# A down GEMM with tokens on the partitions of its result: final norm per partition, residual brought into token order by transfers and VectorE transposes

## The chip, the cores and the metric

The kernel runs on one core of one Trainium2 chip. The metric is the device time of one execution in microseconds (us); lower is better. A core has TensorE (PE; its weight loads are listed as PEld), VectorE (DVE), ScalarE (ACT), GpSimd (POOL), and SyncE (SP), which here only issues transfers. SBUF and PSUM have 128 partitions; a PSUM bank holds 512 float32 values in each partition.

## The reference

The reference computes one step of a one-layer encoder for 1024 prompt tokens and 8 x 16 sample tokens, 1152 in all, with a model width of 1024. The first half of the layer mixes three branches and adds the normed result to the input, which gives `x`. What matters here is the second half:

```python
def rmsnorm(x, g):
    xf = x.astype(F32)
    y = xf * lax.rsqrt(jnp.mean(xf * xf, axis=-1, keepdims=True) + EPS)
    return (y * g.astype(F32)).astype(x.dtype)
...
    h2 = rmsnorm(x, p['g_pre2'])
    f, conv_new = conv_ffn(h2, conv_buf, p['w_ffn_up'], p['w_dw'], p['b_dw'], p['w_ffn_down'])
    x = x + rmsnorm(f, p['g_post2'])
```

`conv_ffn` projects up to 2 x 2816 columns, applies a causal convolution of width 3, GELU and a gate, and projects down again: `act @ w_ffn_down`, a product of 1152 x 2816 by 2816 x 1024. All is float32, and the norm's mean is taken over the 1024 model columns of one token.

## The kernel before

**Layout.** Nearly everything is kept with features on the partitions and tokens along the free axis. The 1152 tokens are three chunks of 384 (`ch(c)`, line 191); the 1024 model columns are eight feature blocks `f` of 128; the 2816 inner columns are 22 blocks `ff`.

**Float32 out of pieces.** A float32 operand is split into a high part, rounded to the format float32r that TensorE multiplies in one pass, and a low part (`split`, line 60: one ScalarE copy and one subtraction on VectorE or GpSimd). `mm3` (line 100) then issues three matmuls: high x high, high x low, low x high. In it, the first operand is the stationary one (128 x 128 weights loaded into TensorE) and the second the moving one, whose columns stream through.

**The up GEMM** (`phase_u`, line 1471). For each `ff` it makes the activation `t` of 128 inner features x 1152 tokens and stores it to the DRAM tile `Dact[ff]` (`up_out`, line 1467). The residual x after the first half, called x2, was stored earlier to the DRAM tile `Dx2[c]`, feature-major (line 1249).

**The down GEMM** (`phase_d`, line 1501). The inner blocks are taken as 2 + 4 x 4 + 4:

- `first()` (line 1649): blocks 0 and 1 for all chunks, with `whole_mm`; the results start the accumulators `M` (seven products) and `y2`.
- four groups of four blocks (`group`, line 1551). For chunks 0 and 1 a group is a 2 x 2 x 2 block product done with seven multiplications (`prod`, line 1615; sums and differences of weight blocks "A" and of activation blocks "B"), and chunk 2 is done plainly (`plain`, line 1632). Each result in PSUM is added into an accumulator in SBUF by `evac` (line 1626), on VectorE. The next group is loaded and split beside it (a Python generator, advanced by `next(nx)`).
- `rest()` (line 1657): the last four blocks, once more with `whole_mm`, in the order chunk 2, 0, 1 and within it over the eight feature blocks (`last_down`, line 1698). Between them the products in `M` are summed into the chunks' results (`sums`, line 1788).

Here the weight slices are stationary (128 inner x 128 model columns) and the activations move (384 tokens), so a result has 128 model columns on its partitions and 384 tokens along the free axis.

**The final norm.** As the model columns lie on the partitions, the sum of squares runs across partitions. `last_down` squares each feature block on ScalarE and adds the squares up on GpSimd; `final_rms` (line 1715) sums over partitions with matmuls against a column of ones and takes the power -1/2 on GpSimd (`rsqrt`, line 79); `row_bcast` (line 88) spreads the 384 factors to all partitions by three diagonal matrices and a matmul with ones; `final_rows` (line 1726) loads x2 in four pieces, multiplies by gain (a value per partition, in `vec`) and by the broadcast row in PSUM, adds x2 on VectorE and GpSimd, and stores `y[c, f]`. For chunks 2 and 0 this goes on beside the matmuls of the next chunk; for chunk 1 it comes after the last matmul. Twelve matmuls whose result is not used (line 1812) stand in the wait.

**What sets the order.** A planner orders each engine's instructions by a simulated timeline: of what is ready by its own estimates it takes the most urgent. `tc.keep_in_program_order` pins an instruction, `tc.high_priority` makes it more urgent, `tc.issue_after(i)` keeps instructions behind `i` on its engine. Nearly all transfers are issued by SP, one queue in order. Results go to eight PSUM banks in turn (`bank`, line 1531).

Of the kernel before, what the change touches and what calls it, by code (L numbers as in the profile page):

```python
# [21 lines left out]
V_PSCALE, V_D, V_WDW, V_BDW, V_GPOST1, V_GPOST2, V_N = 52, 54, 58, 124, 146, 154, 162  # L22
# [9 lines left out]
class K:  # L32
# [75 lines left out]
    def consts(self):  # L108
# [9 lines left out]
        nc.gpsimd.memset(self.mhalf, -0.5)  # L118

# [1347 lines left out]
    def up_out(self, s):  # L1467
        self.nc.vector.tensor_mul(s.t, s.t, s.g)
        self.nc.sync.dma_start(self.Dact[s.ff], s.t)

    def phase_u(self):
        for s in self.first:
# [28 lines left out]
    def phase_d(self):  # L1501
# [6 lines left out]
        with ExitStack() as ctx:  # L1508
            def pool(name, bufs):
                return ctx.enter_context(tc.tile_pool(name=name, bufs=bufs, reuse_waits="tile"))  # L1510
            P = _Multi(pool("d", 1), {"sq": pool("dsq", 3), "tmp": pool("dtm", 2), "dB": pool("db", 1)})
# [19 lines left out]
            def bank():  # L1531
                self.nb += 1
                return (self.sm() if self.nb % 2 else self.pc())[:, 0:384]
# [81 lines left out]
            def prod(s, p):  # L1615
# [16 lines left out]
            def plain(s, f):  # L1632
                b = bank()
                fs = slice(f % 4 * 128, f % 4 * 128 + 128)
                for k in range(4):
                    ah, al = s.A[("A11", "A12", "A21", "A22")[f // 4 * 2 + k // 2]]
                    self.mm3(b, ah[:, k % 2, fs], al[:, k % 2, fs], s.c[:, 0, k], s.c[:, 1, k], k == 0, k == 3)
                evac(False, y2[:, f], b)
# [46 lines left out]
            def whole_mm(ss, c, f, pin=False):  # L1685
                b = bank()
                fs = slice(f * 128, f * 128 + 128)
                for i, s in enumerate(ss):
                    self.mm3(b, s.wh[:, fs], s.wl[:, fs], s.hi[:, self.ch(c)], s.lo[:, self.ch(c)],
# [3 lines left out]
            def row(c, f):  # L1693
                if c == 2:
                    return y2[:, f]
                return M[((2, 4), (3, 5))[c][f // 4]][:, f % 4]

            def last_down(last, c, f, acc, end):

                b = whole_mm(last, c, f, True)  # L1700
                y = row(c, f)
                self.evac = V.tensor_add(y, y, b)
                tc.keep_in_program_order(self.evac)
                if f == 0:
                    nc.scalar.activation(acc[0], y, AF.Square)
                    return
                sq = P.tile([128, 384], F32, tag="sq", name="sq")
                nc.scalar.activation(sq, y, AF.Square)
                if end and f > 5:
                    acc.append(sq)  # L1710
                else:
                    with tc.high_priority():
                        G.tensor_add(acc[0], acc[0], sq)

            def final_rms(acc):
                ss = self.sm()[:, 0:3]
                for i, s in enumerate(acc):
                    for t in range(3):
                        m = nc.tensor.matmul(ss[:, t:t + 1], s[:, t * 128:t * 128 + 128], self.ones[:, 0:1],
                                             start=(i, t) == (0, 0), stop=(i, t) == (len(acc) - 1, 2))  # L1720
                        if i + t == 0:
                            tc.keep_in_program_order(m)
                with tc.high_priority():
                    return self.rsqrt(P, ss, 3)

            def final_rows(c, rs, i):

                with tc.high_priority():
                    rb = self.row_bcast(P, rs, 3, self.pc(), pin=True)
                order = tc.keep_in_program_order  # L1730
                yield
                for f in range(0, 8, 2):
                    if i == 2:
                        x2 = self.rawtile([128, 2, 384], "x2r")
                    else:
                        x2 = self.w2.tile([128, 2, 384], F32, tag="w", name="x2r")
                    nc.sync.dma_start(x2, self.Dx2[c, f:f + 2].rearrange("f p n -> p f n"))
                    y = [row(c, f), row(c, f + 1)]
                    for k in range(2):
                        order(V.scalar_tensor_tensor(y[k], y[k], self.vec[:, V_GPOST2 + f + k:V_GPOST2 + f + k + 1],  # L1740
                                                     rb, op0=OP.mult, op1=OP.mult))
                    order(V.tensor_add(y[0], y[0], x2[:, 0, :]))
                    (V if (i, f) == (3, 6) else G).tensor_add(y[1], y[1], x2[:, 1, :])
# [251 lines left out]
```

## Time and profile before

| | |
|---|---|
| median of 3 runs | 1547.19 us (1545.49 to 1548.5) |
| profiled execution, its own time | 1548.72 us |
| its span, first to last instruction | 1546.9 us |
| mean granted TensorE clock | 0.993 |
| transfers | 183.51 MB, 109,263 packets, mean 119 GB/s |
| last stage (`whole_mm` of the last four blocks) | first matmul at 1477.24 us, last at 1530.46 us |

Times within the profile count from the span's start. A busy share is an engine's time with at least one instruction at work, and a matmul's recorded length overlaps the next one's start, so the pace of matmuls is read from their starts. "Chain" on the page is the work that ended last, followed back from the end:

```profile
PE 83%; DVE 7%; DMA 4%; ACT 3%; issue 2%; POOL 0%; DVEq 0%; ACTq 0%; SPq 0%; POOLq 0%
```

### The profile page before, as it was taken

Reading aid. Unit: us, or ns where it says so; the run is one execution under the profiler, and the core shown is the slowest. Engines: PE = TensorE matmul, PEld = TensorE weight load, DVE = VectorE, ACT = ScalarE, POOL = GpSimd, SP = SyncE. Lnnn points to the kernel's source line nnn. Section 1 sums busy time; section 2 is a strip of 40 time slices with the busy share of each in tenths; the row PEclk is TensorE's granted clock in tenths of the full one; section 3 lists DMA queues with packets and bytes.
Section 4 is the critical chain, followed back from the end, with each engine's and each line's share of the span. In section 5 each row is a group of like instructions: output and inputs, shape, how many; then the busy total and the mean of one; then the engine's idle time right before and its main releaser. Section 6 shows DMA issues by size and latency. Waiting matters only on the chain.

```text
span 1546.9 us, 23088 instructions
## 1 busy us (share of the span) xinstructions
PE 1524.9 (99%) x8914; PEld 1489.2 (96%) x8914; DVE 1097.8 (71%) x1714; ACT 627.4 (41%) x960; POOL 451.4 (29%) x429
## 2 busy tenths in 40 slices
PE   9999999999999899999999999999999999999997
PEld 7999998889999899999999999999999999999997
DVE  7956987796788666637587566566566569888876
ACT  8313445373655224435454343333333343333322
POOL 0000010000012343300046344344344301565545
PEclk9999999999999999999999999999999999999998
DMA  7533334554345873513313221221221233222324
GB/s 270 171 103 103 109 117 161 166 217 125 103 155 171 250 218 103 156 36 123 126 50 117 72 93 70 72 85 57 74 84 57 84 109 133 75 102 98 93 73 167
DMA packets 109263, 183.51 MB, mean 119 GB/s; under 512 B 24417, under 2 KB 76769, under 8 KB 109153
## 3 DMA queue, kind: packets, MB, share of 16 engines
q1 hardware_dynamic: 108576, 181.54, 35.4%
q8 instruction: 70, 1.15, 0.3%
q10 hardware_dynamic: 576, 0.49, 0.1%
q14 instruction: 41, 0.33, 0.1%
HBM read 134.27 MB, written 47.73 MB: 118 GB/s over the span
## 4 chain that ended last, share of the span: by engine, by line
PE 83%; DVE 7%; DMA 4%; ACT 3%; issue 2%; POOL 0%; DVEq 0%; ACTq 0%; SPq 0%; POOLq 0%
PE pc L106 14%; PE pc L102 14%; PE pc L105 14%; PE ps L102 11%; PE ps L105 11%; PE ps L106 11%; DMA Ts<-DG 1%; PE ps L854 1%; DMA DG<-gs 1%; ACT hhi L125 1%; DVE dB L63 1%; PE ps L768 1%; DVE mg L1265 1%; PE ps L1212 0%; PE ps L820 0%
## 5 line engine op out<-in xcount | busy, mean ns | idle before, releaser
L105 PE MATMUL pc<-hlo,whi 128*128 128x384 f32 x504 | 171.8, 341 | 0.3 <-DVE hlo L126 0.3
L102 PE MATMUL pc<-hhi,whi 128*128 128x384 f32 x504 | 171.7, 341 | 0.0
L106 PE MATMUL pc<-hhi,wlo 128*128 128x384 f32 x504 | 169.9, 338 | 0.5 <-DVE wlo L63 0.5
L63 DVE TENSOR_TENSOR wlo<-rawt,whi 128x1024 fp32r<-128x1024 f32 (+1 forms) x99 | 123.0, 1243 | 54.1 <-ACT whi L62 53.8
L62 ACT ACTIVATE whi<-rawt 128x1024 fp32r<-128x1024 f32 (+1 forms) x99 | 103.3, 1044 | 124.8 <-PE pc L105 71.5
L62 ACT ACTIVATE S<-S 128x512 fp32r<-128x512 f32 x112 | 69.9, 629 | 163.8 <-PE ps L106 87.0
L63 DVE TENSOR_TENSOR S<-S,S 128x512 fp32r<-128x512 f32 x112 | 88.9, 798 | 54.9 <-ACT S L62 52.8
L106 PE MATMUL pc<-h2hi,wlo 128*128 128x384 f32 x352 | 119.1, 338 | 0.0
L105 PE MATMUL pc<-h2lo,whi 128*128 128x384 f32 x352 | 118.4, 336 | 0.5 <-DVE h2lo L63 0.5
L102 PE MATMUL pc<-h2hi,whi 128*128 128x384 f32 x352 | 118.5, 337 | 0.0
L102 PE MATMUL ps<-bT,S 128*128 128x384 f32 x304 | 101.7, 334 | 0.0
L105 PE MATMUL ps<-bT,S 128*128 128x384 f32 x304 | 101.7, 334 | 0.0
L106 PE MATMUL ps<-bT,S 128*128 128x384 f32 x304 | 101.7, 334 | 0.0
L105 PEld LDWEIGHTS pc<-hlo,whi 128*128 128x128 f32 x504 | 94.7, 188 | 3.7 <-DVE hlo L126 1.0
L106 PEld LDWEIGHTS pc<-hhi,wlo 128*128 128x128 f32 x504 | 94.7, 188 | 2.9 <-DVE wlo L63 1.2
L102 PEld LDWEIGHTS pc<-hhi,whi 128*128 128x128 f32 x504 | 94.8, 188 | 1.9 <-issue 0.6
L62 ACT ACTIVATE dhi<-dwr 128x1024 fp32r<-128x1024 f32 x38 | 39.6, 1057 | 83.9 <-PE pc L105 49.3
L102 PE MATMUL ps<-ohi,whi 128*128 128x384 f32 x192 | 65.6, 342 | 3.7 <-DVE sgl L1158 2.7
L105 PEld LDWEIGHTS pc<-h2lo,whi 128*128 128x128 f32 x352 | 66.0, 188 | 0.8 <-DVE h2lo L63 0.8
L106 PEld LDWEIGHTS pc<-h2hi,wlo 128*128 128x128 f32 x352 | 66.2, 188 | 0.0
L102 PEld LDWEIGHTS pc<-h2hi,whi 128*128 128x128 f32 x352 | 66.1, 188 | 0.0
L85 POOL TENSOR_TENSOR rs_y<-rs_v,mhalf 128x3 f32<-128x3 f32 (+1 forms) x13 | 14.0, 1081 | 177.2 <-ACT rs_v L83 177.2
(494 smaller groups left out, 4610.8 us busy)
## 6 DMA issues: line engine op xcount, KB each, us to landing
rawt<-in_w_up SPq DMA_DIRECT2D x44, 512.0 KB, 3.4
rawt<-in_w_gate SPq DMA_DIRECT2D x40, 512.0 KB, 3.8
Dsg<-sg SPq DMA_DIRECT2D x72, 192.0 KB, 1.9
sgl<-Dsg SPq DMA_DIRECT2D x72, 192.0 KB, 3.2
Dact<-t SPq DMA_DIRECT2D x22, 576.0 KB, 3.7
dwr<-in_w_down SPq DMA_DIRECT2D x22, 512.0 KB, 3.5
xT<-in_xT SPq DMA_DIRECT2D x20, 384.0 KB, 7.7
dBr<-Dact SPq DMA_DIRECT2D x8, 768.0 KB, 5.2
```

Source lines behind the costliest of these rows:

```text
L62: a = nc.scalar.activation(hi, src, AF.Copy)
L63: return a, (eng or nc.vector).tensor_sub(lo, src, hi)
L85: nc.gpsimd.tensor_tensor(y, v, self.mhalf[:, 0:n], op=OP.pow)
L102: i = nc.tensor.matmul(out, whi, xhi, start=start, stop=False)
L105: nc.tensor.matmul(out, whi, xlo, start=False, stop=False)
L106: nc.tensor.matmul(out, wlo, xhi, start=False, stop=stop)
L125: a = nc.scalar.activation(hi[:, k, :], x[:, k, :], AF.Copy, scale=g)
L768: nc.tensor.matmul(od[:, b, hp, :], cv[:, b % 2, m, hp * 128:hp * 128 + 128], PT[:, 2 * (b // 4) + hp, m, 32 * (b % 4):32 * (b % 4) + 32], ...
L854: nc.tensor.matmul(o, va[:, m, 2 * hp + e, :], pT[:, m, :], start=m == 0, stop=m == 1)
L1265: V.scalar_tensor_tensor(oT[:, f, :], oT[:, f, :], self.vec[:, V_GPRE2 + f:V_GPRE2 + f + 1], rb, op0=OP.mult, op1=OP.mult)
```

## The change

The roles in `mm3` are exchanged throughout the down GEMM: slices of the activations (128 inner x 128 tokens) are stationary and the weights (512 model columns) move. A result has 128 tokens on its partitions and 512 model columns along the free axis: half `h` of token tile `t` of chunk `c`. `prod`, `plain`, `evac`, `whole_mm`, the accumulators and the initial loop follow.

The final norm is then per partition. `square` lets ScalarE square a half and sum it along the free axis (`accum_out`), and turns it into mean + EPS with a second small instruction whose bias is the value of the half before. GpSimd takes the power of one value per partition. The gain is now along the free axis: `g2`, loaded once, 128 equal rows, multiplied in on GpSimd (the last half on VectorE). One VectorE instruction per half multiplies by the factor and adds x2. The last half of the last tile is done in two pieces of 256 columns.

x2 must come in token order. During the up GEMM `x2_blocks` copies `Dx2` to a new DRAM tile `Dx2b`, two copies in each of 18 steps, 36 in all, each 128 KB in runs of 32 tokens; `x2_load` loads a token tile of it and transposes it in blocks of 32 x 32 on VectorE. `final_rms`, `final_rows` and the twelve unused matmuls go. The layout of the output `y` and its rearrangement on the host follow.

```diff
+        self.eps = c.tile([128, 1], F32, name="eps")
+        nc.gpsimd.memset(self.eps, EPS)
...
-        self.nc.sync.dma_start(self.Dact[s.ff], s.t)
+        self.act_out = self.nc.sync.dma_start(self.Dact[s.ff], s.t)
+
+    def x2_blocks(self, n):
+
+        c, t, a = n // 12, n // 4 % 3, n % 4
+        D = self.Dx2[c].rearrange("f p n -> (f p) n").rearrange("(b i) n -> i b n", i=32)
+        at = t * 128 + 32 * a
+        self.nc.sync.dma_start(self.Dx2b[c, t, a].rearrange("i (b j) -> i b j", b=32), D[:, :, at:at + 32])
...
                 self.up_last(cur, "a")
+                with self.tc.issue_after(self.act_out.ins):
+                    for n in range(2 * ff - 6, min(2 * ff - 4, 36)):
+                        self.x2_blocks(n)
...
-            P = _Multi(pool("d", 1), {"sq": pool("dsq", 3), "tmp": pool("dtm", 2), "dB": pool("db", 1)})
+            P = _Multi(pool("d", 1), {"sq": pool("dsq", 2), "dB": pool("db", 1)})
+            g2 = P.tile([128, 1024], F32, tag="g2", name="g2")
+            nc.sync.dma_start(g2, self.I["g2"])
...
-                for f in range(4):
-                    fs = slice(f * 128, f * 128 + 128)
+                for t in range(3):
+                    ts = slice(t * 128, t * 128 + 128)
                     b = bank()
                     for k in range(2):
-                        self.mm3(b, ah[:, k, fs], al[:, k, fs], bh[:, k, :], bl[:, k, :], k == 0, k == 1)
-                    evac(s.g == 0 and p in (1, 5, 6), M[p][:, f], b)
+                        self.mm3(b, bh[:, k, ts], bl[:, k, ts], ah[:, k, :], al[:, k, :], k == 0, k == 1)
+                    evac(s.g == 0 and p in (1, 5, 6), M[p][:, t], b)
...
+            def x2_load(c, t):
+
+                r = self.rawtile([128, 1024], "x2b")
+                nc.sync.dma_start(r, self.Dx2b[c, t].rearrange("a i n -> (a i) n"))
+                x2 = self.w2.tile([128, 1024], F32, tag="w", name="x2r")
+                V.transpose(x2, r)
+                return x2
+
+            def square(y, bias):
+
+                sq = P.tile([128, 512], F32, tag="sq", name="sq")
+                n = y.shape[1]
+                a = small("ss")
+                nc.scalar.activation(sq[:, 0:n], y, AF.Square, accum_out=a)
+                v = small("rs_v")
+                nc.scalar.activation(v, a, AF.Identity, scale=1.0 / 1024, bias=bias)
+                return v
+
+            def last_down(c, t, x2, end):
+
+                v = self.eps
+                yg = []
+                for h in range(2):
+                    y = row(c, h)[:, t]
+                    for cols in (slice(0, 256), slice(256, 512)) if end and h else (slice(0, 512),):
+                        b = whole_mm(cur, c, t, h, True, cols)
+                        self.evac = V.tensor_add(y[:, cols], y[:, cols], b)
+                        tc.keep_in_program_order(self.evac)
+                        v = square(y[:, cols], v)
+                    g = g2[:, 512 * h:512 * h + 512]
+                    if end and h:
+                        z = P.tile([128, 512], F32, tag="yg", name="yg")
+                        V.tensor_mul(z, y, g)
+                        y = z
+                    else:
+                        G.tensor_mul(y, y, g)
+                    yg.append(y)
                 with tc.high_priority():
-                    rb = self.row_bcast(P, rs, 3, self.pc(), pin=True)
...
+                    r = small("rs_y")
+                    G.tensor_tensor(r, v, self.mhalf[:, 0:1], op=OP.pow)
+                for h in range(2):
+                    V.scalar_tensor_tensor(yg[h], yg[h], r, x2[:, 512 * h:512 * h + 512], op0=OP.mult, op1=OP.add)
+                    (nc.scalar if end and h else nc.sync).dma_start(self.O["y"][3 * c + t][:, 512 * h:512 * h + 512], yg[h])
...
+            sums = {(2, 0): ((G, 2, 1), (V, 6, 1)), (2, 1): ((V, 4, 6),), (2, 2): ((V, 4, 7),), (0, 0): ((V, 5, 6),),
+                    (0, 1): ((V, 3, 5),), (0, 2): ((G, 5, 7),)}
+            tiles = [(c, t) for c in (2, 0, 1) for t in range(3)]
+            x2 = [x2_load(*tiles[i]) for i in range(2)]
+            for i, (c, t) in enumerate(tiles):
+                if i + 2 < len(tiles):
+                    x2.append(x2_load(*tiles[i + 2]))
+                last_down(c, t, x2[i], i == len(tiles) - 1)
+                for e, p, q in sums.get((c, t), ()):
+                    e.tensor_add(M[p], M[p], M[q])
```

More of the change, by code (lines that the diff above doesn't have):

```diff
@@ L1690, in whole_mm, with row @@
                              i == 0, i == len(ss) - 1, pin and i == 0)
                 return b
-            def row(c, f):
+            def row(c, h):
                 if c == 2:
[L1695 to L1722, printed above, removed]
-                with tc.high_priority():
-                    return self.rsqrt(P, ss, 3)
@@ L1726, in final_rows @@
-            def final_rows(c, rs, i):
-                with tc.high_priority():
-                    rb = self.row_bcast(P, rs, 3, self.pc(), pin=True)
[L1730 to L1743, printed above, removed]
-                    for k in range(2):
-                        nc.sync.dma_start(self.O["y"][c, f + k], y[k])
-                    yield
+                    return y2[:, :, 512 * h:512 * h + 512]
@@ new lines, in row, with small @@
+                return M[((2, 4), (3, 5))[c][h]]
+            def small(name):
+                return P.tile([128, 1], F32, tag=name, name=name, bufs=3)
+            def x2_load(c, t):
[12 more added lines that the diff above has]
+                return v
@@ L1752, in phase_d @@
             Mt = [self.mtile([128, 2, 4, 384], F32, f"M{i}") for i in range(4)]
+            Mt = [t.rearrange("p i f n -> p (i f n)").rearrange("p (i t n) -> p i t n", i=2, t=3) for t in Mt]
             M = {p: Mt[(p - 1) // 2][:, (p - 1) % 2] for p in range(1, 8)}
[L1754 to L1758 removed]
+            y2 = self.mtile([128, 3, 1024], F32, "y2")
+            for c, h, p in ((0, 0, 2), (1, 0, 3), (1, 1, 7), (0, 1, 4), (2, 0, 0), (2, 1, 0)):
+                for t in range(3):
+                    b = whole_mm(cur, c, t, h)
                     if p == 4:
[L1760 removed]
+                        V.tensor_sub(M[4][:, t], b, M[7][:, t])
                     else:
[L1762 removed]
+                        evac(True, M[p][:, t] if p else row(2, h)[:, t], b)
                 next(nx, None)
@@ L1773, in phase_d @@
                 prod(cur, 2)
-                for f in range(8):
-                    plain(cur, f)
-                    if f % 4 == 3:
-                        next(nx, None)
+                for h in range(2):
+                    for t in range(3):
+                        plain(cur, t, h)
+                    next(nx, None)
                 for p in (3, 4, 5, 6, 7):
@@ L1783, in phase_d @@
                 cur = new
-            accs = Mt[3][:, 1].rearrange("p (c k) n -> p c k n", c=2)
-            acc = [[accs[:, i % 2, 0]] for i in range(3)]
-            rows = iter(())
-            sums = {(0, 0): ((G, 2, 1), (V, 6, 1)), (0, 1): ((V, 4, 6),), (0, 3): ((V, 4, 7),), (0, 4): ((V, 5, 6),),
-                    (0, 6): ((V, 3, 5),), (0, 7): ((G, 5, 7),)}
-            order = (2, 0, 1)
-            for i, c in enumerate(order):
-                for f in range(8):
-                    last_down(cur, c, f, acc[i], i == 2)
-                    for e, p, q in sums.get((i, f), ()):
-                        e.tensor_add(M[p], M[p], M[q])
-                    if i:
-                        if f == 1:
-                            rs = final_rms(acc[i - 1])
-                        elif f == 3:
-                            rows = final_rows(order[i - 1], rs, i)
-                            next(rows)
-                        if 2 < f < (7 if i == 1 else 6):
-                            next(rows)
-            with tc.issue_after(self.evac.ins):
-                rs = final_rms(acc[2])
-                for _ in rows:
-                    pass
-            b = bank()
-            s = cur[0]
-            for _ in range(12):
-                tc.keep_in_program_order(nc.tensor.matmul(b, s.wh[:, 0:128], s.hi[:, 0:384], start=True, stop=True))
-            for _ in final_rows(order[2], rs, 3):
-                pass
+            sums = {(2, 0): ((G, 2, 1), (V, 6, 1)), (2, 1): ((V, 4, 6),), (2, 2): ((V, 4, 7),), (0, 0): ((V, 5, 6),),
[8 more added lines that the diff above has]
+                    e.tensor_add(M[p], M[p], M[q])
 class _S:
@@ L1888, in _layout @@
         cols(a["pool_scale"]), cols(a["ssm_d"][0][perm]), cols(a["w_dw"]), cols(a["b_dw"]),
-        cols(a["g_post1"]), cols(a["g_post2"])], axis=1))
+        cols(a["g_post1"])], axis=1))
+    o["g2"] = c(np.tile(a["g_post2"].reshape(1, 1024), (128, 1)))
     cst = np.zeros((128, C_N), f)
@@ L1960, in _unlayout @@
     y = np.empty((NT, 1024), np.float32)
-    y[_rows()] = r["y"].transpose(0, 3, 1, 2).reshape(NT, 1024)
+    y[_rows()] = r["y"].reshape(NT, 1024)
     mk = r["mk"].reshape(2, 64, 2, 256).transpose(3, 2, 0, 1)
```

32 lines of the change are left out of this document (14 added, 18 removed).

## The prediction

> **What bounds the kernel now.** I read the page's busy shares first, then the table of stretches over the down GEMM, then the timeline of the end. Columns of the stretches: start and end, length, then busy us and instruction count of PE, PEld, DVE, ACT and POOL, granted clock, DMA share, GB/s.
>
> ```profile
> PE 1524.9 (99%) x8914; PEld 1489.2 (96%) x8914; DVE 1097.8 (71%) x1714; ACT 627.4 (41%) x960; POOL 451.4 (29%) x429
> ...
> 1290.00:1300.00 10.00, 9.17 (x53) 8.69 (x51) 10.00 (x17) 4.33 (x5) 0.00 (x0) 1.00 0.00 0
> 1300.00:1335.00 35.00, 34.35 (x195) 33.96 (x195) 29.01 (x40) 9.96 (x10) 11.44 (x6) 1.00 0.38 129
> ...
> 1477.20:1530.60 53.40, 53.30 (x306) 52.10 (x305) 36.69 (x51) 14.04 (x31) 35.47 (x29) 1.00 0.30 96
> 1530.60:1546.90 16.30, 6.65 (x34) 5.95 (x32) 8.70 (x17) 2.21 (x6) 6.13 (x6) 0.68 0.39 147
> ```
>
> TensorE never stops before 1530.6 us, but for 0.8 us and 0.65 us in 1290 to 1335, where VectorE was busy without a break (10.00 of 10). So in the down GEMM only TensorE's own time counts, and after 1530.6 a chain of small steps, 16.3 us long. Its main steps, from the timeline (start, length, engine):
>
> ```profile
> 1530.46 0.33 PE L106 MATMUL pc<-act,dlo 128*128 128x384 f32 x1
> ...
> 1530.83 0.55 DVE L1702 TENSOR_TENSOR M<-M,pc 128x384 f32<-128x384 f32 x1 [0.32 <-PE pc L106]
> ...
> 1531.47 0.52 ACT L1708 ACTIVATE sq<-M 128x384 f32<-128x384 f32 x1 [0.35 <-DVE M L1702]
> ...
> 1532.92 0.17 ACT L83 ACTIVATE rs_v<-ps 128x3 f32<-128x3 f32 x1 [0.92 <-PE ps L1719]
> 1533.73 0.85 POOL L85 TENSOR_TENSOR rs_y<-rs_v,mhalf 128x3 f32<-128x3 f32 x1
> 1534.62 0.99 ACT L93 ACTIVATE diag<-ident,rs_y 128x128 f32<-128x128 f32 x3 [1.53 <-POOL rs_y L85]
> 1536.47 0.81 PE L95 MATMUL pc<-diag,ones 128*128 128x384 f32 x2
> 1537.32 1.14 DVE L1740 SCALAR_TENSOR_TENSOR M<-M,vec,pc 128x384 f32<-128x384 f32 x2 [4.42 <-PE pc L95]
> ...
> 1543.40 0.55 DVE L1743 TENSOR_TENSOR M<-M,x2r 128x384 f32<-128x384 f32 x1
> ```
>
> After the last matmul come the square, column sums on TensorE, the power, three diagonals, a broadcast matmul, and 6.6 us of VectorE over a whole chunk of 384 tokens (1537.32 to 1543.95). From there to the end of the span, 1546.9, it is 2.95 us (the last store and the program's close).
>
> **The matmul stream.** The old form has 1488 matmuls with a moving operand of 384 columns (144 in the first two feature blocks, 264 in each of four groups, 288 in the last four blocks). The new one has 1116 of 512: the same 571,392 columns. So all hangs on whether a matmul has a fixed cost. Starts of back-to-back matmuls at three widths:
>
> ```profile
> 75.26 0.28 PE L102 MATMUL ps<-whi,mhi 128*128 128x256 f32 x1
> ...
> 76.70 0.28 PE L102 MATMUL ps<-whi,mhi 128*128 128x256 f32 x1
> ...
> 321.70 0.40 PE L847 MATMUL ps<-at 128*128 128x512 f32 x1
> ...
> 322.64 0.34 PE L105 MATMUL pc<-hlo,whi 128*128 128x384 f32 x1
> ...
> 323.86 0.33 PE L106 MATMUL pc<-hhi,wlo 128*128 128x384 f32 x1
> ...
> 378.32 0.39 PE L848 MATMUL ps<-at,at 128*128 128x512 f32 x1
> ...
> 379.93 0.34 PE L102 MATMUL pc<-hhi,whi 128*128 128x384 f32 x1
> ```
>
> Between the first pair lie 12 steps of 256 columns, 0.120 us each. From 322.64 to 323.86 are 7 steps of 384: 0.174. From 321.70 to 322.64 are 4 steps of 512 (0.235), from 378.32 to 379.93 seven (0.230): 0.232 over the eleven. Per column 0.453 ns at 384 and 0.453 at 512: 1488 x 0.174 = 258.9 us and 1116 x 0.232 = 258.9 us. I take **0**. The bounds: a straight line through 256 and 384 gives 0.228 at 512, 254.4 us, 4.5 saved; at 0.235 it is 262.3, 3.4 lost. The last half tile in two pieces of 256 costs 24 x 0.120 - 12 x 0.232 = 0.1 more.
>
> The Trainium skill, "TensorE: Matmul & The Clock Gate", section "Back-to-back issue gap", gives columns / 2.4 + 2.5 ns: by it (an estimate) 0.1625 and 0.216, and a gain of 1.0 us. The trace's 0.174 and 0.232 do not agree with it.
>
> **Norm work taken out of the stream.** For chunks 2 and 0 the column sums and the broadcast sat between matmuls of the last stage:
>
> ```profile
> 1498.32 0.34 PE L106 MATMUL pc<-act,dlo 128*128 128x384 f32 x1
> ...
> 1499.55 0.34 PE L106 MATMUL ps<-act,dlo 128*128 128x384 f32 x1
> ...
> 1503.20 0.34 PE L106 MATMUL pc<-act,dlo 128*128 128x384 f32 x1
> ...
> 1504.19 0.33 PE L105 MATMUL ps<-act,dhi 128*128 128x384 f32 x1
> ```
>
> Three ordinary steps took 1.23 us in place of 0.52, and two took 0.99 in place of 0.35: 1.35 us for a chunk. Two chunks: **-2.7**. Nothing replaces it on TensorE, as the sum of squares now comes out of ScalarE's accumulator.
>
> **The prices of the new small steps.** Rows by form (busy us, mean ns):
>
> ```profile
> L580 DVE TENSOR_TENSOR V<-ar,ps 128x512 f32<-128x512 f32 x4 | 2.7, 684 | 0.1
> L1628 DVE COPY M<-ps 128x384 f32<-128x384 f32 x12 | 6.6, 550 | 5.3 <-PE pc L106 5.3
> L63 DVE TENSOR_TENSOR wlo<-rawt,whi 128x1024 fp32r<-128x1024 f32 x97 | 121.6, 1254 | 48.9 <-ACT whi L62 48.5
> L855 DVE RECIPROCAL yt<-ps 64x512 f32<-64x512 f32 x8 | 26.8, 3355 | 1.8 <-PE ps L854 1.6
> L62 ACT ACTIVATE S<-S 128x512 fp32r<-128x512 f32 x112 | 69.9, 629 | 163.8 <-PE ps L106 87.0
> L1399 POOL TENSOR_TENSOR S<-rawt 128x512 f32<-128x512 f32 x19 | 25.6, 1348 | 124.3 <-PE ps L106 124.3
> L1795 POOL TENSOR_TENSOR M<-M 128x1536 f32<-128x1536 f32 x1 | 4.2, 4211 | 0.0
> ```
>
> Taking a result out of PSUM costs VectorE 0.684 at 512 (first row) against 0.550 at 384, so 18 where 24 stood save 24 x 0.550 - 18 x 0.684 = 0.9 us of VectorE in the first stage, where it starved TensorE for 1.5. I take half of it: **-0.4**, between -1.5 (stall gone) and +1.5 (the planner's new order stalls as much again).
>
> **The new end.** Stream end to first step: 1530.46 + 0.174 = 1530.63, so 0.20 to 1530.83. Then, for a last piece of 256 columns: add out of PSUM 0.42 (0.684 and 0.550 carried on to 256); hand-over 0.09 and square 0.42 (from 0.629 and 0.52); the mean with bias 0.10 + 0.17; power 0.10 + 0.85; two final multiply-adds of 512 columns 0.05 + 2 x 0.684. That is 3.8, and with the 2.95 after VectorE's last step 6.7 us. The multiplication of the last half by the gain (VectorE) lies beside the square.
>
> What may be late is GpSimd's queue. A tile of 128 tokens lasts 24 x 0.232 = 5.57 us of TensorE. GpSimd does two gain multiplications and a power in it: 2 x 1.348 + 0.85 = 3.55. The final multiply-add now reads two operands from SBUF, where the old one read the broadcast from PSUM, and such a step does not run beside GpSimd:
>
> ```profile
> 1525.95 1.02 POOL L1713 TENSOR_TENSOR M<-M,sq 128x384 f32<-128x384 f32 x1 [0.52 <-ACT sq L1708]
> ...
> 1526.16 1.23 DVE L1742 TENSOR_TENSOR M<-M,x2r 128x384 f32<-128x384 f32 x1
> ...
> 1532.35 0.55 DVE L1742 TENSOR_TENSOR M<-M,x2r 128x384 f32<-128x384 f32 x1
> ```
>
> The same addition took 0.55 alone and 1.23 where GpSimd was already at work. So the two share 3.55 + 2 x 0.684 = 4.92 of the 5.57. The sum of M5 and M7 on GpSimd, 4.2 us, falls after the sixth of nine tiles, and three tiles recover only 3 x 0.65 = 1.95: some 2.5 us are still owed at the last tile. The tail is then 9.2, between 6.7 (nothing owed) and 12. Against 16.3: **-7.1**, between -9.6 and -4.3.
>
> The Trainium skill, "SBUF — State Buffer", section "SBUF: two separate sides", calls this an exclusive lock held for a whole instruction by a VectorE step with two SBUF inputs or by GpSimd; the 1.23 agrees.
>
> **The transposes.** Nine of 128x1024 on VectorE; the trace has none. Between 1.25 us (the 1024-wide subtraction) and 6.7 (twice the 512-wide reciprocal, the dearest form per column). I take 1.25, as the nearest in kind: each element is read and written once. VectorE then has 2 x 0.684 + 1.25 + 2 x 0.684 = 4.0 a tile, within 5.57, and its sums are done ahead as now; eight PSUM banks, 2.8 us of TensorE each, cover a late one. So 0.
>
> The Trainium skill, "Vector Engine (DVE) Microarchitecture Reference", section 3.8, has a transpose at one element per cycle and lane, at 0.96 GHz an estimated 1.07 us; no run here shows it, and by it the sum is the same.
>
> **The transfers.** 36 copies of 128 KB from DRAM to DRAM in pieces of 128 bytes, two in each of 18 steps of the up GEMM; then nine loads of 512 KB in place of twelve of 384, and one of 512 KB for the gain.
>
> ```profile
> DG<-gs SPq DMA_DIRECT2D x4, 64.0 KB, 3.3
> ...
> 1018.32 0.33 SPq L1469 DMA_DIRECT2D Dact<-t  x1
> 1028.25 0.33 SPq L67 DMA_DIRECT2D rawt<-in_w_up  x1
> ```
>
> The nearest, 64 KB in small pieces, lands in 3.3 us, so two copies are done within 3.3 to 13 us. SP's queue is empty for 10 us behind the store of `Dact` where they go, and they wait for a store of x2 hundreds of us old. Only the next weight load could be held, by 3 us at most, while TensorE is at the products of the block before (it shows no idle time in these stretches): 0. Without that cover each of the 18 steps would pay up to 3 us; I leave that out of the range. The gain's load goes where tiles of the up GEMM lay; should it be queued ahead of the loads behind it, it would hold them, which I price in the range alone.
>
> **Sum.** -2.7 - 7.1 - 0.4 + 0.1 = -10.1. The profiled execution took 1548.72 (span 1546.9), so 1538.6; that run lies 1.5 above the median, 1547.19, and from the median it is **1537.1 us**.
>
> **The rivals.**
> 1. *A fixed cost per matmul* (0.228 at 512): 4.5 more is saved, 1532.6. For it: 256 columns cost 0.469 ns each. Against: the eleven steps of 512. Chance 0.15.
> 2. *GpSimd and VectorE take the tail's place*: the lock and the sums leave 6 us or more owed at the last tile, so that the tail stays at 12 to 16 and little but the norm work is won: 1543, between 1540 and 1547. For it: only 0.65 of 5.57 spare. Against: GpSimd kept up with 35.47 of 53.40 before. Chance 0.18, one half within 0.2% of before.
> 3. *VectorE becomes the bound of the last stage*: transposes at 6.7 make 9.4 a tile, 3.9 over, and nine tiles 35 us, all at the end, as the banks only put it off: 1572. All gains are gone at 10.1 / 9 = 1.1 over, which is a transpose of 3.9 us. For it: no row of a transpose, and the reciprocal shows that a VectorE step can cost five times another. Against: it does no arithmetic. Chance 0.12, slower.
> 4. The forecast: 0.55.
>
> A measurement of this kernel tells about 0.2% (3 us) from no change. Faster: 0.55 + 0.15 + half of 0.18 less a little = 0.78; same 0.10; slower 0.12. The range: low end 1537.1 - 4.5 (stream) - 2.5 (nothing owed) - 1.1 (stall gone) = 1529; high end + 3.4 + 2.8 + 1.9 (first stage) = 1545.2, set to 1546 for part of rival 2.
>
> **What would show it.** Steps of 512 columns at 0.232 in the down GEMM; no gap in the last stage's matmuls; under 10 us from the last matmul to the end; transposes near 1.25; unchanged stretches of the up GEMM. I am wrong if TensorE waits in the last stage for PSUM, if the transposes take over 2.8 us (5.57 less the other steps, 4 x 0.684), or if the planner orders the first stage so that weights come late.

## The result and the profile after

The changed kernel takes 1539.22 us (median of 4 runs, 1536.95 to 1539.43), the kernel before 1547.10 in the runs beside it (1545.49 to 1548.5). The ratio is 0.9944, with a 95% interval from 0.9929 to 0.9958: 8 us faster. The forecast was 1537.1. So the total came out close, but not by the parts that were forecast.

The profiled execution of the changed kernel took 1536.95 us, 2 us less than its other three runs. Two executions differ by some microseconds already before the stages that were changed (the twelve traces reach the same matmul between 783.5 and 788.7 us), so all comparisons of traces below count from one matmul, the first of the up GEMM that reads `h2hi`. From the timeline of TensorE of before, then of after (start, length, engine and line):

```profile
788.28 0.34 PE L102 MATMUL pc<-h2hi,whi 128*128 128x384 f32 x1
```

```profile
784.95 0.34 PE L102 MATMUL pc<-h2hi,whi 128*128 128x384 f32 x1
...
1518.35 0.28 PE L106 MATMUL ps<-dhi,act 128*128 128x256 f32 x1
```

From there to the last matmul are 1530.46 - 788.28 = 742.18 us before and 1518.35 - 784.95 = 733.40 after: **the stream of matmuls lost 8.8 us**, where the forecast had 3.0. From the last matmul to the end of the span are 1546.9 - 1530.46 = 16.4 before and 1535.2 - 1518.35 = 16.8 after: **the tail lost nothing**, where the forecast had 7.1. Together they are 8.4 us, close to the 7.9 of the medians.

The stretches of after, with the columns of the stretches of before. The first two held TensorE's gaps before; the third is the turn from the groups to the last stage, which TensorE begins at 1468.57; the fourth is the rest of that stage, the fifth what follows the last matmul:

```profile
1290.00:1300.00 10.00, 10.00 (x46) 8.29 (x45) 10.00 (x14) 0.85 (x1) 0.00 (x0) 1.00 0.40 138
1300.00:1335.00 35.00, 35.00 (x154) 28.53 (x153) 29.97 (x37) 11.65 (x12) 17.95 (x8) 1.00 0.26 89
...
1463.00:1479.00 16.00, 16.00 (x71) 12.97 (x70) 15.73 (x17) 1.17 (x1) 0.00 (x0) 1.00 0.56 193
1479.00:1518.50 39.50, 39.50 (x184) 32.67 (x182) 34.98 (x34) 13.63 (x42) 29.09 (x21) 1.00 0.29 109
1518.50:1535.20 16.70, 0.13 (x2) 0.00 (x0) 7.39 (x12) 4.00 (x15) 6.38 (x7) 0.64 0.25 95
```

TensorE (first pair) has no gap left, neither at 1290 to 1335 nor in the last stage. VectorE (third pair) has none either from 1463 to 1479, 15.73 of 16: it enters the last stage late, and takes the stage's first result out of PSUM 8.1 us behind the last matmul of that result (bare of the norm, 4.1). In the kernel before it was 3.8 us behind there, and had caught up by the sixth feature block (0.4). What it does in the tail is seen in the timeline of the end (in brackets the idle time before an instruction, and who ended it):

```profile
1519.16 0.55 POOL L1757 TENSOR_TENSOR rs_y<-rs_v,mhalf 128x1 f32<-128x1 f32 x1
1519.74 1.41 DVE L1759 SCALAR_TENSOR_TENSOR M<-M,rs_y,x2r 128x512 f32<-128x512 f32 x2 [2.65 <-POOL rs_y L1757]
1521.08 0.68 DVE L1744 TENSOR_TENSOR M<-M,ps 128x512 f32<-128x512 f32 x1
1521.67 0.68 DVE L1744 TENSOR_TENSOR M<-M,pc 128x512 f32<-128x512 f32 x1
1521.79 0.63 ACT L1731 ACTIVATE sq<-M 128x512 f32<-128x512 f32 x1 [3.61 <-DVE M L1744]
...
1522.59 2.48 POOL L1753 TENSOR_TENSOR M<-M,g 128x512 f32<-128x512 f32 x2 [2.88 <-ACT sq L1731]
...
1525.03 0.54 POOL L1757 TENSOR_TENSOR rs_y<-rs_v,mhalf 128x1 f32<-128x1 f32 x1
1525.61 1.41 DVE L1759 SCALAR_TENSOR_TENSOR M<-M,rs_y,x2r 128x512 f32<-128x512 f32 x2 [3.26 <-POOL rs_y L1757]
...
1527.87 0.42 DVE L1744 TENSOR_TENSOR M<-M,ps 128x256 f32<-128x256 f32 x1
...
1530.10 0.54 POOL L1757 TENSOR_TENSOR rs_y<-rs_v,mhalf 128x1 f32<-128x1 f32 x1
1530.67 0.75 DVE L1759 SCALAR_TENSOR_TENSOR M<-M,rs_y,x2r 128x512 f32<-128x512 f32 x1 [1.66 <-POOL rs_y L1757]
1531.34 0.74 DVE L1759 SCALAR_TENSOR_TENSOR yg<-yg,rs_y,x2r 128x512 f32<-128x512 f32 x1
```

Read it from below. The last sum out of PSUM starts at 1527.87, 9.5 us behind the last matmul (1518.35), which before took 0.37 us (1530.46 to 1530.83). From that sum to the end of the span are 7.3 us: the chain that the forecast had put at 6.7. So the new chain is as short as was thought, but it starts late, since VectorE is late. Why is seen further up: the final multiply-adds (L1759) of a tile stand in VectorE's queue ahead of the next tile's sums (L1744), and wait there, 2.65 and 3.26 us, for the power on GpSimd (L1757), which itself stands behind two multiplications by the gain (L1753). The sums that wait behind release ScalarE's square, this releases GpSimd's multiplications, and these the next power: a ring. Its turn is 1525.61 - 1519.74 = 5.87 us, longer than a tile of TensorE (24 steps of 0.2306 us here, 5.53 us).

This order stands only at the end. The planner put the multiply-adds of the first three tiles behind both sums of the next tile, here those of the third tile:

```profile
1498.30 0.65 DVE L1744 TENSOR_TENSOR M<-M,ps 128x512 f32<-128x512 f32 x1
1498.88 0.68 DVE L1744 TENSOR_TENSOR M<-M,pc 128x512 f32<-128x512 f32 x1
1499.47 2.43 DVE L1759 SCALAR_TENSOR_TENSOR y<-y,rs_y,x2r 128x512 f32<-128x512 f32 x2
```

Those of the fourth to sixth tile stand between the two sums, those of the seventh and eighth ahead of both. VectorE's lag behind TensorE at a tile's first sum fell from 11.3 us at the third tile to 8.0 at the sixth, and rose again to 11.6 at the ninth.

The forms of the last stage of after, from 1479 on (busy us, mean ns | idle before and by whom it was ended):

```profile
L1753 POOL TENSOR_TENSOR M<-M,g 128x512 f32<-128x512 f32 x11 | 15.4, 1411 | 13.5 <-ACT sq L1731 13.5
L1753 POOL TENSOR_TENSOR y<-y,g 128x512 f32<-128x512 f32 x6 | 11.7, 1959 | 34.4 <-ACT sq L1731 34.4
L1759 DVE SCALAR_TENSOR_TENSOR y<-y,rs_y,x2r 128x512 f32<-128x512 f32 x6 | 10.6, 1799 | 1.1 <-POOL rs_y L1757 1.1
L1759 DVE SCALAR_TENSOR_TENSOR M<-M,rs_y,x2r 128x512 f32<-128x512 f32 x11 | 9.8, 931 | 9.5 <-POOL rs_y L1757 9.5
L1723 DVE STREAM_TRANSPOSE x2r<-x2b 128x1024 f32<-128x1024 f32 x5 | 6.2, 1241 | 0.1
```

A transpose takes 1.24 us. A final multiply-add takes 0.74 us alone (the row of 1531.34) and 1.80 in the mean of the first three tiles, where GpSimd is at work beside it. VectorE waits 9.5 + 1.1 us for the power.

### The profile page after: what moved, and what is told of

Same layout as the page of the kernel before. It is cut to its first block, busy times and chain, and to the rows that moved or that the text cites. A ratio compares the mean times of both kernels' runs of the same rounds, so it can differ in the third digit from the quotient of the medians.

```text
span 1535.2 us, 22221 instructions
## 1 busy us (share of the span) xinstructions
PE 1510.2 (98%) x8506; PEld 1430.9 (93%) x8506; DVE 1100.4 (72%) x1658; ACT 629.7 (41%) x981; POOL 441.2 (29%) x423
## 4 chain that ended last, share of the span: by engine, by line
PE 78%; DVE 9%; DMA 4%; ACT 3%; issue 3%; POOL 3%; SPq 0%; DVEq 0%; POOLq 0%; ACTq 0%
PE pc L102 14%; PE pc L106 14%; PE pc L105 14%; PE ps L102 11%; PE ps L105 11%; PE ps L106 11%; DMA Ts<-DG 1%; PE ps L856 1%; DMA DG<-gs 1%; ACT hhi L127 1%; DVE M L1645 1%; POOL dlo L63 1%; DMA sgl<-Dsg 1%; PE ps L770 1%; DVE y L1759 1%
## 5 line engine op out<-in xcount | busy, mean ns | idle before, releaser
L63 DVE TENSOR_TENSOR wlo<-rawt,whi 128x1024 fp32r<-128x1024 f32 (+1 forms) x99 | 123.3, 1246 | 53.3 <-ACT whi L62 53.0
L102 PE MATMUL pc<-mhi,whi 128*128 128x384 f32 x192 | 65.5, 341 | 0.0
```

Source lines behind the costliest of these rows:

```text
L63: return a, (eng or nc.vector).tensor_sub(lo, src, hi)
L102: i = nc.tensor.matmul(out, whi, xhi, start=start, stop=False)
```

## The experiments

Two theories for the tail. **Order** (the expectations call it the waiting theory): VectorE is late because of what waits in its queue for GpSimd. **Work**: VectorE and GpSimd simply have too much to do in the last stage. Two for the stream: its pace depends on the **width** of a matmul alone, or on something that the norm's work does **beside** it. Each run was timed against the kernel before on the same chip; that median moved between 1545.56 and 1547.10 us from one set of runs to the next, so times of different sets are compared by their ratios, or by stream and tail in the traces.

### The final multiply-adds behind the next tile's sums

```diff
+                def fin():
                     for h in range(2):
                         V.scalar_tensor_tensor(yg[h], yg[h], r, x2[:, 512 * h:512 * h + 512], op0=OP.mult, op1=OP.add)
...
-                last_down(c, t, x2[i], i == len(tiles) - 1)
+                f = last_down(c, t, x2[i], i == len(tiles) - 1)
+                if i:
+                    with tc.issue_after(self.evac.ins):
+                        fin()
+                fin = f
```

> The changed kernel with one order pinned: the final multiply-adds of a token tile are queued on VectorE behind the next tile's last addition out of PSUM, not ahead of it. Same work. Waiting theory (VectorE stands in its queue for the power of the tile at hand, so that each tile takes it 5.7 to 5.9 us against TensorE's 5.5, and a lag of 9.5 us is still there at the last tile): the lag of the last addition behind its matmul falls from 9.5 us to 3 or less, time 1531 to 1534. Work theory (VectorE and GpSimd have too much to do, in part one after the other at the shared SBUF port): the lag stays at 8 or more, time 1537 to 1540.

Measured: 1532.55 us (1531.84 to 1533.98), ratio 0.9911 (0.9894 to 0.9928). From the last stage's timeline and forms of this run:

```profile
1508.86 1.25 DVE L1723 STREAM_TRANSPOSE x2r<-x2b 128x1024 f32<-128x1024 f32 x1
...
1510.03 0.65 DVE L1744 TENSOR_TENSOR M<-M,ps 128x512 f32<-128x512 f32 x1
1510.60 0.68 DVE L1744 TENSOR_TENSOR M<-M,pc 128x512 f32<-128x512 f32 x1
...
1511.20 2.44 DVE L1761 SCALAR_TENSOR_TENSOR M<-M,rs_y,x2r 128x512 f32<-128x512 f32 x2
...
1513.67 1.25 DVE L1723 STREAM_TRANSPOSE x2r<-x2b 128x1024 f32<-128x1024 f32 x1
```

```profile
L1761 DVE SCALAR_TENSOR_TENSOR M<-M,rs_y,x2r 128x512 f32<-128x512 f32 x11 | 13.9, 1301 | 0.5 <-POOL rs_y L1757 0.5
```

The wait for the power is 0.5 us in place of 9.5, and no bracket with idle time stands in these rows of VectorE. A tile takes it 1513.67 - 1508.86 = 4.81 us, 0.7 less than TensorE, so it catches up tile by tile: the last sum is 3.5 us behind the last matmul, not 9.5 (3 or less was expected), and the tail 11.2 us, not 16.8. The order of one queue was worth 5.6 us of tail; the medians lie 6.7 us apart, the ratios 0.0033, which is 5.1 us. What remains, 3.5 us, is work: the multiply-adds have become longer, 1.30 for 0.93, as they now always run beside GpSimd's multiplications.

### The transposes left out

```diff
-                x2 = self.w2.tile([128, 1024], F32, tag="w", name="x2r")
-                V.transpose(x2, r)
-                return x2
+                return r
```

> The changed kernel without its nine VectorE transposes: the residual is added as it was loaded, in block order, so the residual part of y is left in the wrong places. Nine times 1.24 us less for VectorE. Waiting theory: the time saved turns into a longer wait for the power, lag 6 to 9 us, time 1536 to 1539. Work theory: the lag falls by most of 9 x 1.24 = 11 us to under 2, time 1530 to 1533.

The residual is then added without being brought into token order. Measured: 1534.46 us (1533.11 to 1535.77), ratio 0.9923 (0.9905 to 0.9941). This lies between the ranges of the two theories. The last sum is 5.0 us behind the last matmul and the tail 12.3 us. Nine transposes are 11.2 us of VectorE, and 4.5 us of the tail hung on them (the medians lie 4.8 us apart, the ratios 3.2). At the start of the last stage VectorE is 4.2 us behind, with them 8.1: four of the nine fall into 1463 to 1479, where it is full (15.73 of 16). So both theories hold in part, and the forecast's "So 0" for the transposes doesn't, though their size was right.

### Both kernels without the final norm

In both, square, mean, power, gain and the addition of x2 are left out, so that the output is the bare sum; the kernel before loses its unused matmuls too.

```diff
-                        v = square(y[:, cols], v)
...
-                    r = small("rs_y")
-                    G.tensor_tensor(r, v, self.mhalf[:, 0:1], op=OP.pow)
...
-                    V.scalar_tensor_tensor(yg[h], yg[h], r, x2[:, 512 * h:512 * h + 512], op0=OP.mult, op1=OP.add)
```

> The changed kernel without final norm, gain and residual: the sums of the down GEMM are stored as y right after the addition out of PSUM (the copies of x2 and the gain's load stay). If the stream's gain is the wider matmul's pace, the norm work taken out and the stalls gone, its last matmul comes where it comes in the changed kernel, 733.5 us after the first matmul of the up GEMM on the second half's input, within 1 us; and the end is 3 to 5 us after it: 1524 to 1528. Whatever lies between that and 1539 is the price of the new final norm.

> The kernel before without final norm, gain and residual, the twelve unused matmuls gone too. Pace theory: its stream still has 1488 matmuls at 0.1743 us against 1116 at 0.2297 and the stalls of the first stage, so it ends 4 to 6 us later than the changed kernel so stripped: 1529 to 1533. If the gain of the stream came from the norm work alone, the two stripped kernels take the same time within 1.5 us.

Measured: the new form 1521.63 us (1520.56 to 1522.57), ratio 0.9839 (0.9823 to 0.9856); the old form 1528.87 (1528.17 to 1529.68), ratio 0.9888 (0.9868 to 0.9907). First and last matmul of the new form, then of the old one:

```profile
785.90 0.34 PE L102 MATMUL pc<-h2hi,whi 128*128 128x384 f32 x1
...
1516.30 0.28 PE L106 MATMUL ps<-dhi,act 128*128 128x256 f32 x1
```

```profile
785.80 0.34 PE L102 MATMUL pc<-h2hi,whi 128*128 128x384 f32 x1
...
1522.54 0.34 PE L106 MATMUL pc<-act,dlo 128*128 128x384 f32 x1
```

The medians lie 7.2 us apart, where 4 to 6 were expected. The streams are 730.40 and 736.74 us: 6.3 us lie between the two forms with no norm in either. All steps of 512 columns in the groups take 0.2267 us (mean over the starts of neighbours), all of 384 take 0.1733. 1116 x 0.2267 = 253.0 against 1488 x 0.1733 = 257.9: 4.9 of the 6.3 are width; 1.9 more are gaps that the old form has without its norm too (0.4 at the end of the first two inner blocks, 1.5 in the first group), and 0.4 go the other way (0.3 in the up GEMM, 0.1 for the pieces of 256).

But the new form's stream is 3.0 us shorter than in the changed kernel (733.40), and this was not expected (733.5 within 1 us was, and 1524 to 1528 for the time): the norm comes after the products. In the changed kernel the steps of 512 come in two kinds:

```profile
1399.62 0.40 PE L102 MATMUL pc<-dhi,dc 128*128 128x512 f32 x1
...
1402.41 0.39 PE L102 MATMUL ps<-dhi,dB 128*128 128x512 f32 x1
...
1405.13 0.39 PE L102 MATMUL ps<-dhi,dB 128*128 128x512 f32 x1
```

Twelve steps lie between the first two rows, 0.2325 us each, and twelve between the second and the third, 0.2267. Sorted by product, the slow ones (0.2334) are those that read a tile in the buffers `dw` or `db`. It makes little difference whether such a buffer holds the moving operand (`dw`, 0.2335 in the mean of 303 steps) or the stationary one (`db`, 0.2331 of 72). These buffers lie behind the small tiles of the norm in SBUF. Nine tiles of 4 bytes, each of which takes 32, move them by 288 bytes a partition against `w1`, `w2` and `act` (the other tiles ahead of them add multiples of 1024); in the bare forms there are no such tiles.

### The place of the buffers

First the changed kernel with its buffers moved back into line, then the bare one with its buffers moved out:

```diff
+            gap = P.tile([128, 112], F32, tag="gap", name="gap")
...
-                return P.tile([128, 1], F32, tag=name, name=name, bufs=3)
+                return P.tile([128, 16], F32, tag=name, name=name, bufs=3)[:, 0:1]
```

> The changed kernel with padding in front of the down GEMM's operand buffers: the small tiles of the norm take 64 bytes a partition instead of 4 and one unused tile of 448 bytes stands before them, so that the buffers dw and db lie 1024 bytes behind their place in the stripped kernel instead of 288 (the buffers that were always at base pace, w1, w2 and act, stay). The order of instructions is meant to stay. Theory A, the place of an operand in SBUF sets a matmul's pace: every step of 512 columns is 0.2267 us as in the stripped kernel (now 0.2267 or 0.2334, mean 0.2297), the stream 1116 x 0.003 = 3.4 us shorter; about 0.7 of it falls in the last stage, where VectorE is behind and the gain is not seen: 1536.5 us, between 1535.3 and 1537.5. Theory B, the slow steps come from the norm's other work (VectorE, ScalarE or transfers beside TensorE): they stay, 1539.2 +- 1.

```diff
+            pads = [P.tile([128, 1], F32, tag="pad", name="pad", bufs=9) for _ in range(9)]
+            for t in pads:
+                G.memset(t, 0.0)
```

> The stripped new form (no square, no mean, no power, no gain, no final multiply-add in the down GEMM, so the output is the bare sum) with nine unused tiles of 4 bytes, each cleared once, in front of dw and db, which moves these by 288 bytes as in the changed kernel. Theory A, place: the steps that read dw or db become 0.2334 instead of 0.2267, the mean 0.2297, and the time 1521.6 + 3.4 = 1525.0 us (1524 to 1526). Theory B, the norm's work slows the steps: no step changes, 1521.6 +- 1.

Measured: moved into line 1536.98 us (1536.06 to 1537.58), ratio 0.9942 (0.9930 to 0.9955); the bare one moved out 1525.26 (1523.04 to 1526.88), ratio 0.9867 (0.9853 to 0.9880). First and last matmul of the two:

```profile
785.92 0.34 PE L102 MATMUL pc<-h2hi,whi 128*128 128x384 f32 x1
...
1516.05 0.28 PE L106 MATMUL ps<-dhi,act 128*128 128x256 f32 x1
```

```profile
787.89 0.34 PE L102 MATMUL pc<-h2hi,whi 128*128 128x384 f32 x1
...
1521.30 0.28 PE L106 MATMUL ps<-dhi,act 128*128 128x256 f32 x1
```

The streams are 730.13 and 733.41 us: the first has the bare form's (730.40), the second the changed kernel's to 0.01 us (733.40). The mean step in the groups goes from 0.2298 to 0.2267 and from 0.2267 to 0.2298. So the place of the operands is the whole of the difference, and the norm's work costs the stream nothing. The first one's time lies in its expected range, but its ratio hardly tells a gain over the changed kernel's (0.9942 against 0.9944), and its trace says why: VectorE does not get faster with TensorE. Its last sum is 11.0 us behind the last matmul instead of 9.5, and the tail 18.5 us instead of 16.8. Of 3.3 us, half was given back, where the expectation had 0.7.

The same for the kernel before, whose four small tiles move `dw` and `db` by 128 bytes (160 past a multiple of 512, the other buffers 32):

```diff
+            gap = P.tile([128, 96], F32, tag="gap", name="gap")
```

> The kernel before with one unused tile of 384 bytes in front of the down GEMM's operand buffers, so that dw and db lie in the same place modulo 512 bytes as w1, w2 and act (160 bytes off in the kernel before). Theory A, place: the steps of 384 columns become 0.17334 us throughout as in its stripped form (mean now 0.1743 to 0.1747), 1488 x 0.0012 = 1.8 us less from the first matmul of the up GEMM to the last of the down GEMM (742.2 to between 740 and 741), 1545 us, which the median can hardly tell from the kernel before. Theory B, only a shift of 288 bytes does it: no change, 742.2.

Measured: 1544.97 us (1542.06 to 1547.43), ratio 0.9990 (0.9980 to 1.0000). First and last matmul of the stream:

```profile
786.66 0.34 PE L102 MATMUL pc<-h2hi,whi 128*128 128x384 f32 x1
...
1527.42 0.33 PE L106 MATMUL pc<-act,dlo 128*128 128x384 f32 x1
```

740.76 us instead of 742.18, and the mean step in the groups 0.1734 instead of 0.1747. The stream shows it; the time does not, its interval reaches 1. The old form too had paid for its buffers' place (its step of 384 rose by 2.7 ns where that of 512 rises by 6.7), and less.

### The gain left out

The output lacks the factor `g2` here; GpSimd keeps the power and its two long sums. VectorE's one multiplication by the gain, in the last half tile, goes too (0.69 us).

```diff
-                    g = g2[:, 512 * h:512 * h + 512]
...
-                        G.tensor_mul(y, y, g)
```

> The changed kernel without the multiplication by the gain g2 in the final norm (two GpSimd multiplications a tile, the last half's on VectorE), so the output lacks the factor g2; everything else stays, the sum of M5 and M7 and that of M2 and M1 on GpSimd too. Theory A (GpSimd's multiplications hold the SBUF port and the power behind them): every final multiply-add but those beside GpSimd's two long sums takes 0.74 us as alone, VectorE needs about 4.1 + 1.2 (wait for the power) = 5.3 us or less a tile against TensorE's 5.5, the lag of the last sum falls from 9.5 to between 3 and 6 us, and the end comes as much earlier: 1539.2 - 5 = 1534 us, between 1532 and 1536.5. Theory B (the lag comes from VectorE's own work and the wait for the mean of the squares, whatever GpSimd does): the multiply-adds stay at 1.8 us in the long form, lag 8 us or more, 1537.5 to 1539.

Measured: 1531.24 us (1530.15 to 1532.62), ratio 0.9900 (0.9885 to 0.9916), below the range of either theory. From the forms of the last stage and the timeline of this run:

```profile
L1752 DVE SCALAR_TENSOR_TENSOR M<-M,rs_y,x2r 128x512 f32<-128x512 f32 x12 | 8.5, 749 | 8.8 <-POOL rs_y L1750 8.7
```

```profile
1507.65 1.42 DVE L1752 SCALAR_TENSOR_TENSOR M<-M,rs_y,x2r 128x512 f32<-128x512 f32 x2 [1.21 <-POOL rs_y L1750]
...
1510.27 0.65 DVE L1744 TENSOR_TENSOR M<-M,pc 128x512 f32<-128x512 f32 x1
1510.84 0.68 DVE L1744 TENSOR_TENSOR M<-M,ps 128x512 f32<-128x512 f32 x1
...
1512.13 0.55 POOL L1750 TENSOR_TENSOR rs_y<-rs_v,mhalf 128x1 f32<-128x1 f32 x1 [4.52 <-ACT rs_v L1733]
...
1512.72 1.41 DVE L1752 SCALAR_TENSOR_TENSOR M<-M,rs_y,x2r 128x512 f32<-128x512 f32 x2 [1.21 <-POOL rs_y L1750]
```

Without GpSimd beside it a multiply-add takes 0.75 (it had 0.93 in the mean, and 1.30 in the late form), and the power is there 1.21 us after VectorE is, at the end 2.31, not 3.26. A tile takes VectorE 1512.72 - 1507.65 = 5.07 us, and the last sum is 1.5 us behind the last matmul. GpSimd's seventeen half-tile multiplications, off every bound by the page's share (POOL is busy 29% of the span), thus cost some 8 us (the tail is 8.7 us, not 16.8): VectorE's multiply-adds add up to 15.6 us instead of 21.1, and its waits for the power to 8.8 instead of 10.6. So the larger part is that multiply-adds are slower beside GpSimd, the smaller part the power that waits behind the multiplications. The Trainium skill, "SBUF — State Buffer", section "SBUF: two separate sides", says that a VectorE step with two SBUF inputs and a GpSimd step that reads SBUF exclude each other for a whole instruction; 0.74 us alone and 1.80 beside it agree.

### The copies issued twice

```diff
-        self.nc.sync.dma_start(self.Dx2b[c, t, a].rearrange("i (b j) -> i b j", b=32), D[:, :, at:at + 32])
+        for o in (self.Dx2b, self.Dx2c):
+            self.nc.sync.dma_start(o[c, t, a].rearrange("i (b j) -> i b j", b=32), D[:, :, at:at + 32])
```

> The changed kernel with each of the 36 copies of x2 from DRAM to DRAM issued twice, the second to a tensor that nobody reads. Theory A, as in the prediction, copies are hidden and cost nothing: 1539.2 +- 1.5, the up GEMM 462 us long as in both kernels. Theory B, they hold the weight loads behind them on SP's queue or on the transfer engines: each of the 18 steps pays up to 3 us once more, 1545 to 1590, and the up GEMM is longer by as much.

Measured: 1536.80 us (1535.35 to 1539.12), ratio 0.9944 (0.9930 to 0.9957), the changed kernel's own (in microseconds it lies below the expected 1539.2 +- 1.5, as the kernel before does beside it). The transfers by line, with KB of one and median us to landing:

```profile
Dx2b<-Dx SPq DMA_DIRECT2D x36, 128.0 KB, 4.4
Dx2c<-Dx SPq DMA_DIRECT2D x36, 128.0 KB, 4.1
```

The second 36 cost nothing that can be measured, so neither do the first. From the first matmul that reads `h2hi` to the first of the down GEMM it is 477.1 us here and in the changed kernel, and 477.3 before.

### All together

The late form, GpSimd's sums given to VectorE, and the buffers in line as above:

```diff
-            sums = {(2, 0): ((G, 2, 1), (V, 6, 1)), (2, 1): ((V, 4, 6),), (2, 2): ((V, 4, 7),), (0, 0): ((V, 5, 6),),
-                    (0, 1): ((V, 3, 5),), (0, 2): ((G, 5, 7),)}
+            sums = {(2, 0): ((V, 2, 1), (V, 6, 1)), (2, 1): ((V, 4, 6),), (2, 2): ((V, 4, 7),), (0, 0): ((V, 5, 6),),
+                    (0, 1): ((V, 3, 5),), (0, 2): ((V, 5, 7),)}
```

> Three edits on the changed kernel: the final multiply-adds of a tile behind the next tile's first sum out of PSUM (the late form, 1532.55 us), the two sums of products M that GpSimd does (3.94 us each) moved to VectorE (1.87 us each in the profile of the changed kernel), and the buffers in the place of the stripped kernel. Theory A (VectorE's lag at the end comes from waits and from GpSimd's long sums that hold its SBUF port, and the pace from the buffers' place): two sums cost VectorE 2 us less each, so the lag of 3.5 us is gone at the last tile, and the stream is 3.4 us shorter: 1532.55 - 3.1 - 3.4 = 1526 us, between 1524.5 and 1528. Theory B (pace not from the place): 1529.4. Theory C (sums no cheaper for VectorE on itself): 1529.2, or 1532.5 with B.

Measured: 1529.23 us (1528.19 to 1531.54), ratio 0.9897 (0.9882 to 0.9912): the fastest full version, 16 us under the kernel before beside it (1545.56). It misses its expectation by 3 us; the number is that of theory C (sums no cheaper for VectorE on itself), and the traces bear this out. The stream is as short as expected (730.09 us), but the last sum is still 3.4 us behind the last matmul. Where the sums went is seen in the timelines of the late form and of this one:

```profile
1488.71 5.69 DVE L1761 SCALAR_TENSOR_TENSOR y<-y,rs_y,x2r 128x512 f32<-128x512 f32 x2 [1.11 <-POOL rs_y L1757]
1489.89 3.96 POOL L1816 TENSOR_TENSOR M<-M,M 128x1536 f32<-128x1536 f32 x1
```

```profile
1483.78 3.47 DVE L1762 SCALAR_TENSOR_TENSOR y<-y,rs_y,x2r 128x512 f32<-128x512 f32 x2 [1.11 <-POOL rs_y L1758]
1487.17 1.75 DVE L1817 TENSOR_TENSOR M<-M,M 128x1536 f32<-128x1536 f32 x1
```

Beside GpSimd's sum a pair of multiply-adds took 5.69 us; without it the pair takes 3.47, and then VectorE has the sum itself, 1.75: 0.5 us less in place of 2. The other sum of GpSimd lies in the groups (at 1438.12 in the changed kernel), where it delayed nothing. And the shorter step helps TensorE get away: a tile is 24 x 0.2267 = 5.44 us now, so that VectorE catches up 0.63 a tile and not 0.72, some 0.7 us less over eight tiles. What holds the end now is VectorE's work there.

## Why the prediction was right in sum and wrong in its parts

- **The pace of matmuls** was taken as 0: mis-sized. With the place of the buffers as they are, the steps from the first start to the last add up to 259.4 us before (144 x 0.1733 + 1056 x 0.1747 + 287 x 0.1741) and 256.3 after (108 x 0.2270 + 792 x 0.2298 + 204 x 0.2306 + 23 x 0.119): -3.1. Of this -4.9 is width, and +1.8 that the new buffers lie worse (3.3 us lost, 1.5 before). The row that failed is that of the attention's matmuls, 0.235 and 0.230 at 512 columns: they read other tiles, and were carried over to a stage where a well-placed step takes 0.2267. The first rival had the mechanism: 0.120, 0.1733 and 0.2267 at 256, 384 and 512 are 13.3 ns fixed and 53.3 ns for each 128 columns. The formula from the Trainium skill, "TensorE: Matmul & The Clock Gate", section "Back-to-back issue gap", has the same slope (128 columns at 2.4 GHz are 53.3 ns) with 2.5 ns fixed; the traces give 13.3, at a granted clock of 1.00. The section gives it for a single matmul by itself, though, and 131 ns at 512 columns for a stream with weight loads, which this stream, at 226.7, does not reach.
- **The norm's matmuls out of the stream**, -2.7: right, a little small. Beyond their plain steps the matmuls of the last stage lost 3.3 us before, in gaps and column sums, and none after.
- **The first stage**, -0.4 with -1.5 as its bound: too small. TensorE's gaps ahead of the last stage, 2.2 us over plain steps, are all gone. That VectorE's busy share made them is not shown: 1300 to 1335 had 29.01 of 35, and after the change VectorE is as busy in both stretches (10.00 and 29.97) with no gap. The one wait that the profile names, 0.83 us before 1291.57, ended with VectorE's copy out of PSUM (L1628); why it is gone was not tried. With 0.3 us in the up GEMM the parts of the stream add up to the 8.8 us.
- **The transfers and the 256-column pieces**: right. **The transposes**: 1.24 us against 1.25, but not free: 4.5 us of tail.
- **The tail**, -7.1: this step failed; it is +0.4, and "under 10 us from the last matmul to the end" came out as 16.8. The chain was right (7.3 us against 6.7). Two things were not. VectorE's sums were to be "done ahead as now", but it entered the last stage 8.1 us late instead of 3.8. And "three tiles recover only 3 x 0.65" failed: the last three tiles recovered nothing (8.0 us behind at the sixth tile's first sum, 9.5 at the end), for 5.57 us of TensorE were set against a sum of busy times, 4.92, where a ring of 5.87 stood. GpSimd's sum of M5 and M7 was expected after the sixth tile; it came after the first, VectorE's lag stood at 11.3 us behind it, at the third tile, and only 3.3 of these were made up by the sixth. The second rival (GpSimd and VectorE take the tail's place, 12 to 16) is what happened in the tail, and a little more of it; it was given 0.18. It, too, counted busy times rather than who stands in front of whom.

So the forecast's time was met by luck: two errors of 6 and 7.5 us, in the stream and in the tail, cancelled.

## What to carry to other kernels

Add up an engine's turn along its waits, not its busy times: an in-order queue in which the last step of one tile stands ahead of the first step of the next makes a ring of all the engines between, and here moving that step behind gained 5.6 us of 1539. An engine with 29% busy can hold the end when it holds another's port and stands ahead of the one small value that everybody waits for. And a faster stream gains only in part where the engine behind it is already late: 1.6 of 3.3 us here.

## What was not expected of the hardware

A float32r matmul whose operand lies in a buffer moved by 288 bytes a partition against the others takes 0.2334 us at 512 columns instead of 0.2267; with a move of 128 bytes (modulo 512), 384 columns take 0.1760 instead of 0.1733; with 1024 bytes (or none) there is no loss. Small tiles of a few bytes ahead of large ones thus cost 3.3 us of stream. Which distance decides, and whether it is that of the two operands or the address itself, was not tried.
